# One more feed-forward pair in block form, filter taps joined over two sequences, and a gate in two operations, in a two-layer diffusion backbone on one Trainium2 core

## The chip, the core and the metric

The kernel runs on one core of a Trainium2 chip. A core has a matrix engine (TensorE, PE in the profile; its weight loads are PEld), a vector engine (VectorE, DVE), a scalar engine (ScalarE, ACT), GpSimd (POOL) and SyncE (SP), which here issues most of the transfers. Each engine runs its own list of instructions in order and waits on semaphores for the others. The metric is the time of one execution on the device in microseconds.

## The reference, cut to what matters

One inference step over 128 prompt tokens and 512 sample tokens, width 1024, two layers. The first layer mixes tokens with a state-space scan, the second with differential attention; after each comes the same feed-forward block:

```python
def dwconv(x, w, b):                 # width 3, centred, zero at both ends, each channel by itself
    ...
def conv_ffn(h, up_w, conv_w, conv_b, down_w):
    u = dwconv(h @ up_w, conv_w, conv_b)      # 1024 -> 2 x 2816
    a, v = jnp.split(u, 2, axis=-1)
    return (jax.nn.silu(a) * v) @ down_w      # 2816 -> 1024
...
xp = xp + p_g2 * conv_ffn(modulate(xp, ...), *ffn_p)   # prompt
xs = xs + s_g2 * conv_ffn(modulate(xs, ...), *ffn_p)   # sample, other shift, scale and gate
```

The filter runs over each sequence by itself: the last sample token must not see the first prompt token, nor the other way round.

## The kernel before

Everything is kept transposed: 128 channels on the partitions, 640 tokens in the columns, columns 0 to 511 the sample, 512 to 639 the prompt. Each float32 operand is split into a rounded high part and a remainder (`hi`, `lo`; `whi`, `wlo` for weights, `mh`, `ml` for the hidden tiles), and each product is three matmuls. ScalarE writes the high part, VectorE the low part (`split_w`, line 262). Weights come in units of 128 x 1024 through a ring of buffers: SP loads `raw`, then comes the cast, one to three units ahead of TensorE.

The hidden width is 22 blocks of 128 rows. For each block the kernel computes a pair: the tile `ua` of the first half and `uv` of the second. `FT` is 22, and `SUB` groups the blocks into three stages: the up-projections of a stage and of one block more, then the down-projection of the stage's blocks into eight output tiles (`po`), each added to the residual `x` with its gate. `MID` is the number of buffers for `mh` and `ml` in each layer.

There are two forms of a pair. In the standard form (`pair` in `ffn`) each tile is 8 blocks of 128 input rows, times three matmuls, times two column parts of 256 and 384. In the block form (`Blocks.pair`) the 2 x 2 blocks of weights and activations are combined so that seven products take the place of eight; each is 4 blocks times three matmuls over 320 columns. It needs sums of activations (`Blocks.sums`, tiles `T`) and sums of weights, which GpSimd forms in DRAM by accumulating transfers (`sum_batch`, tensor `wsum`), a batch of blocks at a time, started by `weight_sums`. The products of a pair go into three PSUM banks `a`, `b`, `c`, parts of the tiles named `ba`, `bb` and `bc`. Products 6 and 7 accumulate into the bank of product 1 after ScalarE has copied it out. Products 3 and 4 of a pair are done during the next pair (`third`, `fourth`), and `fourth` ends with the epilogue. `STD` is the number of pairs in standard form: 16 in the first layer, 5 in the second, so 6 and 17 in block form.

The epilogue of a pair filters `ua` into `ca` and `uv` into `cv`, applies SiLU to `ca`, multiplies, and splits the product into `mh` and `ml`. The filter (`conv`, line 677) is one ScalarE operation over 640 columns with the middle tap as scale and the bias, then four VectorE operations: left and right tap, for the sample and for the prompt.

`gate_add` (line 403) adds an output tile to the residual in three VectorE operations, of 256, 256 and 128 columns, because `project_out` calls it for two column parts, "A" and "B", and "B" holds two gates. `project_last` does the last stage's projection and starts the next norm; at the end of a layer it needs the last pair's `mh` and `ml` for its first two tiles' last steps.

In the first layer's feed-forward VectorE also computes the second layer's modulation (`mod_rest`, tiles `mw` and `junk`), which is drained before the down-projection that follows the last standard pair; during that down-projection it makes the sums of activations.

The order on each engine is fixed when the program is built: a list scheduler of the framework takes the instructions in program order as priority, but lets a later one go first if it expects it to be ready sooner.

Of the kernel before, what the change touches and what calls it, by code (L numbers as in the profile page):

```python
# [9 lines left out]
F32 = mybir.dt.float32  # L10
# [16 lines left out]
A0, A1, B1 = 0, 256, 640  # L27
PO = 256
HALF = {"A": (A0, A1), "B": (A1, B1), "C": (0, 384), "D": (384, 640)}
COL0 = {"A": PO, "B": PO, "C": 128, "D": 128}  # L30
COND = {"A": ((0, 256, 1),), "B": ((256, 512, 1), (512, 640, 0)),
        "C": ((0, 384, 1),), "D": ((384, 512, 1), (512, 640, 0))}
# [12 lines left out]
SUMS = 3  # L45
ATT_SPLIT = 6
NF = 19
RSQRT_MAGIC = float(0x5F3759DF)
# [119 lines left out]
class Step:  # L168
# [516 lines left out]
    def ffn(self, l, h, nextnorm, pool):  # L685
# [5 lines left out]
        def copy_out(ps):  # L691
# [2 lines left out]
            self.act(u, ps[:, PO:PO + T], AF.Copy)  # L694
            return u

        def epilogue(p, ua, uv):
            ca = self.tmp("ca")
            self.conv(ca, ua, cw[:, p, :])
            cv = self.tmp("cv")  # L700
            self.conv(cv, uv, cw[:, FT + p, :])
            self.act(ca, ca, AF.Silu)
            self.tt(cv, ca, cv, ALU.mult)
            hi = self.slot("mh", f"mh{p}", F32R, bufs=MID[l], pool=pool)
            lo = self.slot("ml", f"ml{p}", F32R, bufs=MID[l], pool=pool)
# [30 lines left out]
        sub = SUB[l]  # L736
        for s, (k0, k1) in enumerate(sub):
            last = s == len(sub) - 1
            self.down = False
            end = min(k1 + 1, FT)  # L740
            while done < end:
                if done >= std:
                    blk.pair(done)
                else:
                    pair(done)
                    if l and done == 0:
                        sums = self.add(blk.sums(), 2)
                done += 1
                if l == 0 and done == 13:
                    self.weight_sums(1, range(STD[1], 11, SUMS), mid[done - 2][0])  # L750
                if l and done == std:
                    self.drain(sums)
                    blk.finish_sums()
            self.down = True
            if l and s == 0:
                self.weight_sums(1, range(14, FT, SUMS), mid[done - 2][0])
# [561 lines left out]
    def weight_units(self):  # L1318
# [10 lines left out]
        def ffn(l):  # L1329
# [8 lines left out]

            done = 0
            out = []  # L1340
            for k0, k1 in SUB[l]:
# [31 lines left out]

    def weight_sums(self, l, starts, mark):

        for p in starts:
            self.sum_batch(l, p, min(p + SUMS, FT), mark.bitcast(F32)[0:1, 0:2])

    def sum_batch(self, l, p0, p1, mark):

# [147 lines left out]
```

## Time and profile before

| | |
|---|---|
| median of 3 runs | 1868.65 us (1864.55 to 1868.84) |
| profiled execution | 1865.84 us |
| its span, first to last instruction | 1864.1 us |
| TensorE busy | 1827.8 us (98%) |
| VectorE busy | 1464.3 us (79%) |
| ScalarE busy | 998.0 us (54%) |
| GpSimd busy | 55.6 us (3%) |

In the profile a line such as "L217 ACT ACTIVATE ca<-ua,fcw 128x640 f32<-128x640 f32 x23 | 21.1, 918 | 29.5" reads: line 217 of the kernel (a helper that issues all ScalarE operations), engine and operation, tile written and tiles read, shapes, how many; busy microseconds in all and mean nanoseconds of one; idle time of the engine ahead of them and what ended it. Since most operations go through helpers, they are told apart by their tiles.

### The profile page before, as it was taken

To read this page: it belongs to the slowest core of one execution; us is meant where nothing else is said; L and a number is where in the kernel's file an instruction comes from. 1 tells how busy PE (TensorE), PEld (TensorE's weight loads), DVE (VectorE), ACT (ScalarE), POOL (GpSimd) and SP (SyncE) were. 2 spreads that over 40 slices of the span, in tenths; PEclk is the share of its full clock that TensorE was granted. 3 is DMA by queue.
4 is the path that set the end of the run, shared out by engine and by line. 5 is a ranking of instruction groups with operands and counts; after the bars stand their busy time and mean duration, and the time that the engine had idled before them with its cause. 6 is when DMAs were issued, how large, how long until landed. Compare 5 with 4: busy or idle time off the path is not lost.

```text
span 1864.1 us, 33068 instructions
## 1 busy us (share of the span) xinstructions
PE 1827.8 (98%) x13057; PEld 1713.0 (92%) x13057; DVE 1464.3 (79%) x2827; ACT 998.0 (54%) x1862; POOL 55.6 (3%) x84
## 2 busy tenths in 40 slices
PE   7999999999999999999999999999999999999996
PEld 4799999989989999999999988888899999999996
DVE  4689999999838999998585877778779874874874
ACT  2479686879426442345363566566536543643641
POOL 0000000000001000011000000000001011100000
PEclk8999999999999999999999999999999999999998
DMA  9734344345546976677742212111047268853421
GB/s 345 249 115 137 105 120 137 114 132 174 172 162 205 271 236 209 200 209 203 209 128 88 88 40 65 57 46 55 21 124 198 93 181 237 256 161 102 142 80 57
DMA packets 108675, 276.06 MB, mean 148 GB/s; under 512 B 12284, under 2 KB 19048, under 8 KB 102504
## 3 DMA queue, kind: packets, MB, share of 16 engines
q1 hardware_dynamic: 100520, 225.19, 37.1%
q0 software_dynamic: 7424, 48.24, 11.1%
q8 instruction: 102, 1.67, 0.4%
q10 hardware_dynamic: 576, 0.52, 0.1%
q14 instruction: 53, 0.43, 0.1%
HBM read 267.95 MB, written 54.19 MB: 173 GB/s over the span
## 4 chain that ended last, share of the span: by engine, by line
PE 92%; DVE 3%; ACT 2%; DMA 2%; issue 1%; SPq 0%; DVEq 0%; ACTq 0%
PE po L226 25%; PE up L226 14%; PE bb L226 6%; PE z L226 6%; PE ba L226 6%; PE bc L226 5%; PE x L226 5%; PE st L226 5%; PE v L226 3%; PE yp L226 3%; PE q L226 2%; PE sl L226 2%; PE k L226 2%; PE ov L226 2%; PE in L226 1%; PE wt L1252 1%
## 5 line engine op out<-in xcount | busy, mean ns | idle before, releaser
L217 ACT ACTIVATE whi<-raw 128x1024 fp32r<-128x1024 f32 (+4 forms) x266 | 270.9, 1020 | 311.3 <-PE po L226 191.4
L223 DVE TENSOR_TENSOR wlo<-raw,whi 128x1024 fp32r<-128x1024 f32 (+4 forms) x266 | 312.2, 1174 | 74.7 <-ACT whi L217 63.2
L220 DVE SCALAR_TENSOR_TENSOR xr<-po,mod,xr 128x256 f32<-128x256 f32 (+2 forms) x231 | 89.0, 433 | 123.9 <-PE po L226 123.8
L226 PE MATMUL po<-ml,whi 128*128 128x256 f32 (+1 forms) x704 | 168.2, 310 | 0.0
L226 PE MATMUL po<-mh,wlo 128*128 128x256 f32 (+1 forms) x704 | 167.9, 310 | 0.0
L226 PE MATMUL po<-mh,whi 128*128 128x256 f32 (+1 forms) x704 | 167.8, 310 | 0.0
L226 PEld LDWEIGHTS po<-mh,whi 128*128 128x128 f32 x704 | 128.1, 188 | 0.8 <-ACT mh L217 0.5
L226 PEld LDWEIGHTS po<-mh,wlo 128*128 128x128 f32 x704 | 128.7, 188 | 0.0
L226 PEld LDWEIGHTS po<-ml,whi 128*128 128x128 f32 x704 | 128.5, 188 | 0.1
L226 PE MATMUL up<-h01h,wlo 128*128 128x256 f32 x464 | 105.7, 309 | 0.0
L226 PE MATMUL up<-h01l,whi 128*128 128x256 f32 x464 | 105.7, 309 | 0.0
L226 PE MATMUL up<-h01h,whi 128*128 128x256 f32 x464 | 105.6, 309 | 0.0
L226 PEld LDWEIGHTS up<-h01h,whi 128*128 128x128 f32 x464 | 84.4, 188 | 0.0
L226 PEld LDWEIGHTS up<-h01h,wlo 128*128 128x128 f32 x464 | 84.4, 188 | 0.0
L226 PEld LDWEIGHTS up<-h01l,whi 128*128 128x128 f32 x464 | 84.4, 188 | 0.0
L217 ACT ACTIVATE mh<-cv 128x640 fp32r<-128x640 f32 x44 | 32.5, 738 | 88.6 <-DVE cv L223 88.6
L217 ACT ACTIVATE e<-sl,sm 128x640 f32<-128x640 f32 x64 | 50.4, 790 | 39.6 <-DVE sm L1189 39.2
L665 DVE CUSTOM_DVE_ANT_0 junk<-mw,cbc 128x1024 bf16<-128x1024 f32 x48 | 58.4, 1217 | 7.4 <-DMA mw<-in_modT 7.1
L226 PE MATMUL z<-h00h,whi 128*128 128x256 f32 (+1 forms) x256 | 63.0, 325 | 0.0
L217 ACT ACTIVATE e<-rb,Ctok 128x128 f32<-128x128 f32 x160 | 56.4, 390 | 12.0 <-issue 9.6
L217 ACT ACTIVATE ca<-ca 128x640 f32<-128x640 f32 x44 | 32.3, 735 | 54.8 <-DVE ca L220 54.6
L226 PE MATMUL bb<-T,whi 128*128 128x320 f32 x264 | 61.6, 313 | 0.0
(580 smaller groups left out, 5309.9 us busy)
## 6 DMA issues: line engine op xcount, KB each, us to landing
wsum<-in_w_blk POOLq DMA_DIRECT2D x42, 768.0 KB, 7.1
raw<-in_w_blk SPq DMA_DIRECT2D x55, 512.0 KB, 3.9
mw<-in_modT SPq DMA_DIRECT2D x48, 512.0 KB, 4.2
raw<-wsum SPq DMA_DIRECT2D x92, 256.0 KB, 2.9
raw<-in_w_in SPq DMA_DIRECT2D x40, 512.0 KB, 5.3
rb<-rowd SPq DMA_DIRECT2D x40, 512.0 KB, 5.5
raw<-in_w_dn SPq DMA_DIRECT2D x32, 448.0 KB, 3.4
raw<-in_w_qkv SPq DMA_DIRECT2D x24, 512.0 KB, 3.3
```

Source lines behind the costliest of these rows:

```text
L217: return self.nc.scalar.activation(out, in_, func, **k)
L220: return self.nc.vector.scalar_tensor_tensor(out, in0, s, in1, op0, op1)
L223: return self.nc.vector.tensor_tensor(out, a, b, op)
L226: return self.nc.tensor.matmul(out, lhsT, rhs, start=start, stop=stop, **k)
L665: nc.vector.tensor_tensor_reduce(w if c else junk, w, cb[:, c, :], 1.0, 0.0, ALU.mult, ALU.add, self.mod[l][:, t, c:c + 1])
L1252: nc.tensor.transpose(pm[:, b * P:(b + 1) * P], ws[b][:, kc * P:(kc + 1) * P], self.ident)
```

## The change

Four things are edited. In the feed-forward filter the left and the right tap are each one VectorE operation over 639 columns, across the border between sample and prompt. What the two taps add wrongly at the border is taken out beforehand on ScalarE: for each of the two border columns one operation forms the bias less the foreign token's share (`edge`, from negated taps `nw`), and one writes that column of the result anew with it. `project_out` calls the gate once, with a new column set "AB" of two parts, 512 and 128. The first layer has 15 standard pairs and 7 block pairs, with stages of 7, 7 and 8 blocks in both layers and 8 buffers for hidden tiles. The weight sums are batched by explicit bounds: the first layer's seven blocks go in batches of 3, 2 and 2. The filter of the state-space layer keeps its four operations.

```diff
-COL0 = {"A": PO, "B": PO, "C": 128, "D": 128}
+COL0 = {"A": PO, "B": PO, "C": 128, "D": 128, "AB": PO}
 COND = {...
+        ... "AB": ((0, 512, 1), (512, 640, 0))}
-SUB = (((0, 8), (8, 15), (15, 22)), ((0, 7), (7, 14), (14, 22)))
-MID = (9, 8)
+SUB = ((0, 7), (7, 14), (14, 22))
+MID = 8
-STD = (16, 5)
+STD = (15, 5)
...
 def project_out(...):
-            for hf in "AB":
-                self.gate_add(i, ps, g, hf)
+            self.gate_add(i, ps, g, "AB")
...
 def ffn(...):
+        def conv(acc, x, t):
+            w, v = cw[:, t, :], nw[:, t, :]
+            self.act(acc, x, AF.Identity, scale=w[:, 1:2], bias=w[:, 3:4])
+            e = pool.tile([P, 2], F32, tag="edge", name="edge", bufs=4)
+            for i, (a, b) in enumerate(((TS - 1, TS), (TS, TS - 1))):
+                self.act(e[:, i:i + 1], x[:, b:b + 1], AF.Identity, scale=v[:, i:i + 1], bias=w[:, 3:4])
+                self.act(acc[:, a:a + 1], x[:, a:a + 1], AF.Identity, scale=w[:, 1:2], bias=e[:, i:i + 1])
+            self.stt(acc[:, 1:T], x[:, :T - 1], w[:, 0:1], acc[:, 1:T], ALU.mult, ALU.add)
+            self.stt(acc[:, :T - 1], x[:, 1:T], w[:, 2:3], acc[:, :T - 1], ALU.mult, ALU.add)
         def epilogue(p, ua, uv):
-            self.conv(ca, ua, cw[:, p, :])
+            conv(ca, ua, p)
-            self.conv(cv, uv, cw[:, FT + p, :])
+            conv(cv, uv, FT + p)
...
+        nw = pool.tile([P, 2 * FT, 2], F32, tag="nw", name=f"nw{l}", bufs=1)
+        for i in range(2):
+            nc.vector.tensor_scalar(nw[:, :, i], cw[:, :, 2 - 2 * i], -1.0, None, ALU.mult)
-        self.weight_sums(l, range(11, 14, SUMS) if l else range(std, FT, SUMS), h[0][0])
+        self.weight_sums(l, (11, 14) if l else (15, 18, 20, 22), h[0][0])
...
 def weight_sums(self, l, starts, mark):
-        for p in starts:
-            self.sum_batch(l, p, min(p + SUMS, FT), ...)
+        for p, q in zip(starts, starts[1:]):
+            self.sum_batch(l, p, q, ...)
```

More of the change, by code (lines that the diff above doesn't have):

```diff
@@ L29 @@
 HALF = {"A": (A0, A1), "B": (A1, B1), "C": (0, 384), "D": (384, 640)}
-COL0 = {"A": PO, "B": PO, "C": 128, "D": 128}
+COL0 = {"A": PO, "B": PO, "C": 128, "D": 128, "AB": PO}
 COND = {"A": ((0, 256, 1),), "B": ((256, 512, 1), (512, 640, 0)),
-        "C": ((0, 384, 1),), "D": ((384, 512, 1), (512, 640, 0))}
+        "C": ((0, 384, 1),), "D": ((384, 512, 1), (512, 640, 0)), "AB": ((0, 512, 1), (512, 640, 0))}
 EPS = 1e-6
@@ L41 @@
 RAW = 4
-STD = (16, 5)
+STD = (15, 5)
 HT = T // 2
 AHEAD = 3
-SUMS = 3
 ATT_SPLIT = 6
@@ L695, in copy_out @@
             return u
+        def conv(acc, x, t):
[7 more added lines that the diff above has]
+            self.stt(acc[:, :T - 1], x[:, 1:T], w[:, 2:3], acc[:, :T - 1], ALU.mult, ALU.add)
         def epilogue(p, ua, uv):
             ca = self.tmp("ca")
-            self.conv(ca, ua, cw[:, p, :])
+            conv(ca, ua, p)
             cv = self.tmp("cv")
-            self.conv(cv, uv, cw[:, FT + p, :])
+            conv(cv, uv, FT + p)
             self.act(ca, ca, AF.Silu)
             self.tt(cv, ca, cv, ALU.mult)
-            hi = self.slot("mh", f"mh{p}", F32R, bufs=MID[l], pool=pool)
-            lo = self.slot("ml", f"ml{p}", F32R, bufs=MID[l], pool=pool)
+            hi = self.slot("mh", f"mh{p}", F32R, bufs=MID, pool=pool)
+            lo = self.slot("ml", f"ml{p}", F32R, bufs=MID, pool=pool)
             self.act(hi, cv, AF.Copy)
@@ L731, in ffn @@
         nc.vector.tensor_scalar(t, t, -1.0, None, ALU.mult)
+        nw = pool.tile([P, 2 * FT, 2], F32, tag="nw", name=f"nw{l}", bufs=1)
+        for i in range(2):
+            nc.vector.tensor_scalar(nw[:, :, i], cw[:, :, 2 - 2 * i], -1.0, None, ALU.mult)
         sums = None
         self.start_tiles(h)
-        self.weight_sums(l, range(11, 14, SUMS) if l else range(std, FT, SUMS), h[0][0])
+        self.weight_sums(l, (11, 14) if l else (15, 18, 20, 22), h[0][0])
         done = 0
-        sub = SUB[l]
+        sub = SUB
         for s, (k0, k1) in enumerate(sub):
@@ L749, in ffn @@
                 if l == 0 and done == 13:
-                    self.weight_sums(1, range(STD[1], 11, SUMS), mid[done - 2][0])
+                    self.weight_sums(1, (5, 8, 11), mid[done - 2][0])
                 if l and done == std:
@@ L755, in ffn @@
             if l and s == 0:
-                self.weight_sums(1, range(14, FT, SUMS), mid[done - 2][0])
+                self.weight_sums(1, (14, 17, 20, 22), mid[done - 2][0])
             if l == 0 and done == std:
@@ L1340, in ffn @@
             out = []
-            for k0, k1 in SUB[l]:
+            for k0, k1 in SUB:
                 end = min(k1 + 1, FT)
@@ L1374, in weight_sums @@
     def weight_sums(self, l, starts, mark):
-        for p in starts:
-            self.sum_batch(l, p, min(p + SUMS, FT), mark.bitcast(F32)[0:1, 0:2])
+        for p, q in zip(starts, starts[1:]):
+            self.sum_batch(l, p, q, mark.bitcast(F32)[0:1, 0:2])
     def sum_batch(self, l, p0, p1, mark):
```

## The prediction

> **What bounds the kernel now.** I read the page's busy shares first, then busy time by stretch, then the waits of TensorE, then single rows around the edits.
>
> ```profile
> span 1864.1 us, 33068 instructions
> ...
> PE 1827.8 (98%) x13057; PEld 1713.0 (92%) x13057; DVE 1464.3 (79%) x2827; ACT 998.0 (54%) x1862; POOL 55.6 (3%) x84
> ```
>
> TensorE is busy 98% of the span, so an edit pays only if TensorE gets less to do or waits less. The next view sums three stretches: 592 to 693 and 754 to 853 us are standard up pairs of the first feed-forward layer, 907 to 972 us block pairs. Columns: window, its length, then PE, PEld, DVE, ACT and POOL busy with their instructions, clock, DMA share, GB/s.
>
> ```profile
> 592.00:693.00 101.00, 101.00 (x690) 101.00 (x689) 96.28 (x160) 50.59 (x63) 7.63 (x10) 1.00 0.87 264
> 754.00:853.00 99.00, 99.00 (x676) 99.00 (x675) 90.28 (x155) 41.65 (x52) 7.14 (x11) 1.00 0.69 205
> 907.00:972.00 65.00, 64.55 (x429) 62.50 (x428) 48.17 (x74) 37.93 (x55) 0.67 (x1) 1.00 0.51 149
> ```
>
> Three things are to be seen. In the standard stretches TensorE never stops, 101.00/690 = 99.00/676 = 0.1464 us for a matmul, although VectorE is full (96.28 of 101) and the DMA engines too (0.87). So VectorE's load there costs nothing now. In block pairs a matmul takes 65.00/429 = 0.1515 us: a pair of 84 matmuls loses 84 x (0.1515 - 0.1464) = 0.43 us, and ScalarE is at 37.93 of 65 there, VectorE at 48.17. What TensorE waits for in block pairs is mostly a ScalarE copy out of PSUM (total, times, longest):
>
> ```profile
> PEld bb L226 <- ACT ua L217: 3.5, 8, 0.9
> ```
>
> **The change part by part.** *The seventh block pair.* A standard pair is 2 tiles x 8 x 3 x 2 = 96 matmuls of 320 columns on average, 96 x 0.1464 = 14.05 us. A block pair is 7 products x 4 x 3 = 84 matmuls, 84 x 0.1515 = 12.73 us with its losses, 84 x 0.1464 = 12.30 without. Gain 1.32 us, at most 1.75. I take 1.32, since the losses lie in all such pairs. The down-projections keep 22 blocks of 128 rows over three stages, so they keep their matmuls; only 8, 7, 7 becomes 7, 7, 8.
>
> The pair also casts 7 half units of weights (512 columns) where a standard pair casts 4, so 1.5 units more on ScalarE and VectorE. In a stretch with 27 us of 65 free on ScalarE and 17 on VectorE this is hidden. On GpSimd's queue a third batch of weight sums (8 transfers and 2 marks) goes out behind the two that end here:
>
> ```profile
> 669.75 0.87 POOL L1384 DMA_DIRECT2D wsum<-in_w_blk  x1 [6.12 <-DMA wsum<-wsum]
> ```
>
> Two batches took from 566 us to this row, about 52 us each, so the third ends near 730 us even at full size, and its first reader comes after 880. It prolongs the crowded DMA time (0.87 in the first stretch), in which TensorE did not stop. SP issues 6 loads for this pair in place of 2. Nothing.
>
> *The order of stages.* The block stage now begins one standard pair (14.05) and 8 x 6 matmuls (7.0 us) sooner. VectorE must have its modulation sums and the block sums of activations ready that much sooner.
>
> ```profile
> 832.95 1.22 DVE L665 CUSTOM_DVE_ANT_0 mw<-mw,cbc 128x1024 f32<-128x1024 f32 x1
> ```
>
> ```profile
> 890.00:900.00 10.00, 4.53 (x8) 1.00 0.85 234
> ```
>
> ```profile
> 902.98 0.30 PE L226 MATMUL ba<-h01h,whi 128*128 128x320 f32 x1
> ```
>
> The last modulation sum ran at 833 us, the activation sums kept VectorE full till about 894.5 us (the second row: VectorE 4.53 of 10), and the first block product came at 902.98: 8.4 us to spare. TensorE will reach the down stage ahead of it at 853 - 21 = 832 us. Even if the modulation sums end no sooner, VectorE enters 2 us behind, within 8.4. Nothing; if that cover were gone, the start of the block stage would slip by what is over.
>
> *Taps over 639 columns.*
>
> ```profile
> L220 DVE SCALAR_TENSOR_TENSOR ca<-ua,fcw,ca 128x511 f32<-128x511 f32 x46 | 34.4, 747 | 12.9 <-ACT ca L217 12.9
> ...
> L220 DVE SCALAR_TENSOR_TENSOR w<-e,sm,e 128x640 f32<-128x640 f32 x32 | 28.1, 880 | 8.6 <-ACT e L217 8.5
> ...
> L220 DVE SCALAR_TENSOR_TENSOR ca<-ua,fcw,ca 128x127 f32<-128x127 f32 x46 | 15.9, 346 | 0.0
> ```
>
> Four operations, 2 x 747 + 2 x 346 = 2186 ns, become two of about 880 (the middle row, one column more). Successive VectorE operations overlap by some 80 ns (four taps last 1.93 us in a row below), so 1.85 becomes 1.60: 0.25 us less for each of 88 filters, 22 us of VectorE in all. It ends no wait of TensorE that the waits name, so by itself it is worth nothing.
>
> *Border columns on ScalarE.* Each filter gets four operations on one column, 88 x 4 = 352 in all. The trace has none of that shape with scale and bias taken from memory.
>
> ```profile
> L217 ACT ACTIVATE uraw<-up 128x640 f32<-128x640 f32 x36 | 24.7, 686 | 0.0
> ...
> L217 ACT ACTIVATE ca<-ua,fcw 128x640 f32<-128x640 f32 x23 | 21.1, 918 | 29.5 <-DVE ua L223 29.5
> ...
> L217 ACT ACTIVATION_READ_ACCUMULATOR e<-sl,sm 128x1 f32 x64 | 12.5, 195 | 0.0
> ...
> L217 ACT ACTIVATE wpT<-wpt 128x128 f32<-128x128 f32 x8 | 2.2, 276 | 0.0
> ```
>
> A column costs (686 - 276)/512 = 0.80 ns, so the filter's own 640-column operation, which has the same two operands, shrinks to 918 - 639 x 0.80 = 407 ns at one column. Less the 0.09 us by which ScalarE operations overlap (0.91 long, 0.82 apart, below) that is 0.31 us in a row. The low end is the one-column row, 195 ns, 0.10 with the overlap; the high end 0.41, if each waits for the one before it, as every second one needs the first's result. I take 0.31, which is of the same kind: 1.24 us a filter, 2.5 a pair, 109 us in all.
>
> The Trainium skill, "ScalarE: Activation LUTs", section "What ACT_TABLE_LOAD costs", gives 186 ns plus about 93 for each operand in memory and 93 of overlap, by which (an estimate) such an operation takes 0.28 us and a pair 2.2; the sum would stay within 0.1 us.
>
> In standard pairs ScalarE has half its time free. In block pairs five pairs lie in 65 us, so its 37.93 becomes 50.6: still below the limit, and I put the steady part at nothing. Its bounds: a gain of 0.43 for each of 23 block pairs (9.9 us), if the waits vanished, and the loss of the first rival.
>
> The cover is gone at the end of a layer, where the last pair's hidden tile is the only thing that TensorE still needs:
>
> ```profile
> 1797.39 0.92 ACT L217 ACTIVATE cv<-uv,fcw 128x640 f32<-128x640 f32 x1
> 1798.22 0.72 ACT L217 ACTIVATE ca<-ca 128x640 f32<-128x640 f32 x1
> 1801.73 0.74 ACT L217 ACTIVATE mh<-cv 128x640 fp32r<-128x640 f32 x1 [2.78 <-DVE cv L223]
> ```
>
> ```profile
> 1798.83 1.93 DVE L220 SCALAR_TENSOR_TENSOR cv<-uv,fcw,cv 128x511 f32<-128x511 f32 x4
> ```
>
> ```profile
> 1802.09 1.30 PE L226 MATMUL po<-mh,whi 128*128 128x256 f32 x6
> ```
>
> The tile `mh` is written at 1801.73 to 1802.47 and TensorE takes it just then. VectorE's taps for `ca` will start 1.24 us later and last 0.25 less, a cast comes between, the taps for `cv` start 1.0 later and last 0.25 less: `mh` comes 0.75 us late, and TensorE with it (bounds 0 and 2.5). In the first layer six more matmuls (0.88 us) now lie ahead of that point, so 0. The two earlier ends of stages in the second layer have cover:
>
> ```profile
> 1511.20 0.82 DVE L223 TENSOR_TENSOR ml<-cv,mh 128x640 fp32r<-128x640 f32 x1
> ```
>
> ```profile
> 1507.97 6.29 PE po L226 x42
> ```
>
> `ml` is done at 1512.0; the last six of these 42 matmuls begin at 1507.97 + 36/42 x 6.29 = 1513.4 and reach `ml` 0.3 later. 1.6 us of cover against 0.75: nothing, or 0.4 each if `ca`'s columns also hold up the copy of `uv`.
>
> *Gate in two operations* for 45 tiles: one operation fewer, its fixed part (346 - 127 x 1.04 = 213 ns, less overlap 0.13 us) on VectorE, behind matmuls that do not wait for it. Nothing. The two small operations for negated taps, once a layer, neither.
>
> **Sum:** -1.32 + 0.75 = -0.6 us. The profiled execution took 1865.84 us (span 1864.1 and 1.7 around it), so 1865.2. It lies 2.8 us under the median of the three runs, by which the sum is 1868.0; I forecast the middle, 1866.6. A difference under 0.3% (5.6 us) cannot be told from none in this kernel.
>
> **The rivals.** *Slower: ScalarE's columns stand ahead of a copy that TensorE needs.* In the second layer's steady pairs:
>
> ```profile
> 1742.85 0.42 ACT L217 ACTIVATE uv<-ba 128x320 f32<-128x320 f32 x1
> 1743.17 0.91 ACT L217 ACTIVATE ca<-ua,fcw 128x640 f32<-128x640 f32 x1
> 1743.99 0.91 ACT L217 ACTIVATE cv<-uv,fcw 128x640 f32<-128x640 f32 x1
> 1744.80 0.41 ACT L217 ACTIVATE ua<-bb 128x320 f32<-128x320 f32 x1
> ```
>
> ```profile
> 1746.06 0.31 PE L226 MATMUL bb<-h11h,whi 128*128 128x320 f32 x1
> ```
>
> The copy `ua<-bb` frees the bank into which the product at 1746.06 goes; it ends at 1745.21, 0.85 us early. Eight columns ahead of it in ScalarE's queue are 2.5 us: TensorE stops 1.6 us. Every second pair has this order, 11 of 23: +18 us, 1884. With four columns ahead, 0.4 x 11 = 4 us, 1871. It decides from 0.5 us of stop in 11 pairs. For it: the slack is one row. Against it: the order is made when the program is built, the copy comes earlier in the program than the columns, so it may go between them. The Trainium skill, same page, section "Rules for kernel authors", sends adds and multiplies to VectorE and budgets some 0.3 us for an operation on ScalarE; by that rule (an estimate) the move is a loss of this kind, and no run here shows it yet.
>
> *Faster: the waits in block pairs go.* If shorter taps freed VectorE's and ScalarE's buffers sooner, half the 0.43 us of 23 pairs would come back, 5 us: 1861.6; all of it 1856.7. Against: the waits name ScalarE's copies, and ScalarE gets more to do.
>
> *The seventh pair brings nothing:* its sums or loads come late and cost the 1.32 us: 1867.9, no change all the same.
>
> **How the numbers follow.** Forecast 0.55, the third case 0.08 (both within 0.3%), slower rival 0.22, faster rival 0.15. So faster 0.15, same 0.63, slower 0.22. The range goes from the faster case's half-way toward all (1859) to a slower case between four and eight columns (1877); that leaves out about 1 in 10. The likeliest alone has 1863 to 1870.
>
> **What would show it.** Right: the first layer has 588 block matmuls in place of 504 and 96 fewer `up`; one-column ScalarE rows near 0.4 us; taps near 880 ns; ScalarE near 1140 us busy (998 + 352 x 0.4), VectorE near 1420 (1464 less 88 x 0.43 and 45 x 0.1); a wait of `po` for `mh` at the end of the second layer of up to 1 us. Wrong: waits of `ba` or `bb` for ScalarE's `ua` far above 3.5 us, a stop before the first block product, or a matmul in block pairs nearer 0.1464 us.

## The result, and the profile after

The changed kernel takes 1878.41 us (median, 1877.56 to 1881.89); the kernel before took 1866.88 on the same chip (1863.62 to 1868.84). The ratio is 1.0066, with an interval from 1.0056 to 1.0077: 11.5 us slower. The forecast was 1866.6, no change, with a range up to 1877. The profiled execution took 1878.28 us.

The page of the changed kernel opens so:

```profile
span 1876.5 us, 33203 instructions
...
PE 1828.7 (97%) x13045; PEld 1711.7 (91%) x13045; DVE 1443.7 (77%) x2615; ACT 1092.0 (58%) x2218; POOL 62.1 (3%) x94
```

TensorE is as long busy as before, 0.9 us more, in a span that is 12.4 us longer: it stops. To find where, I take the first matmul of each normalisation, `st`, on the feed-forward's input (`h01h`), on the attention's (`h10h`) and on the second feed-forward's (`h11h`), and the end of the span. These are starts of single rows, 569.1, 1031.3 and 1399.4 us before, 570.1, 1042.0 and 1409.8 after.

| Stretch | before | after |
|---|---|---|
| first feed-forward (`h01h` to `h10h`) | 462.2 | 471.9 |
| attention (`h10h` to `h11h`) | 368.1 | 367.8 |
| second feed-forward (`h11h` to the end) | 464.7 | 466.7 |

So 9.7 us of the loss lie in the first feed-forward and 2.0 in the second. The waits of TensorE in the first, from 560 to 900 us (total, times, longest), a view that is empty for the kernel before:

```profile
PE po L225 <- ACT mh L216: 4.8, 2, 3.2
PE po L225 <- DVE ml L222: 1.6, 1, 1.6
PE po L225 <- DVE xr L219: 1.5, 1, 1.5
PE po L225 <- ACT uraw L216: 0.5, 1, 0.5
```

These are 8.4 us, all of `po`, the down-projection, and most for hidden tiles, `mh` and `ml`. In the timeline of TensorE they stand at the first down-projection (692 and 694 us) and at the second. The second begins 16 us sooner than it did; its first row before:

```profile
853.18 0.45 PE L226 MATMUL po<-mh,whi 128*128 128x256 f32 x2
```

and after, with the longest stop:

```profile
837.22 0.56 PE L225 MATMUL po<-mh,whi 128*128 128x256 f32 x2 [0.50 <-ACT uraw L216]
...
845.95 0.90 PE L225 MATMUL po<-mh,whi 128*128 128x256 f32 x2 [3.19 <-ACT mh L216]
```

The same hidden tile on VectorE, from the timeline of that engine:

```profile
826.94 0.88 DVE L219 SCALAR_TENSOR_TENSOR cv<-uraw,fcw,cv 128x639 f32<-128x639 f32 x1
831.89 1.22 DVE L663 CUSTOM_DVE_ANT_0 junk<-mw,cbc 128x1024 bf16<-128x1024 f32 x1 [4.06 <-DMA mw<-in_modT]
833.04 0.82 DVE L222 TENSOR_TENSOR cv<-ca,cv 128x640 f32<-128x640 f32 x1
...
834.92 1.22 DVE L663 CUSTOM_DVE_ANT_0 junk<-mw,cbc 128x1024 bf16<-128x1024 f32 x1
...
836.06 0.82 DVE L222 TENSOR_TENSOR ml<-cv,mh 128x640 fp32r<-128x640 f32 x1
836.80 0.88 DVE L219 SCALAR_TENSOR_TENSOR ca<-uraw,fcw,ca 128x639 f32<-128x639 f32 x1
...
842.41 1.80 DVE L219 SCALAR_TENSOR_TENSOR cv<-uraw,fcw,cv 128x639 f32<-128x639 f32 x2 [0.63 <-ACT cv L216]
...
845.93 0.83 DVE L222 TENSOR_TENSOR ml<-cv,mh 128x640 fp32r<-128x640 f32 x1 [0.86 <-ACT mh L216]
```

VectorE has the second tap of `cv` done at 827.8 and the gated half `ca` has been there since 822.6 (ScalarE's timeline below, under e4). But the next instruction in its queue is a modulation reduction, and its tile of weights, `mw`, lands only at 831.9. VectorE stands still for 4.06 us with the hidden tile's work behind it. The load itself was issued only at 827.1 us, when VectorE had read out one of the two buffers of `mw` (a reduction from 825.80, 1.22 us long), and took 4.8 us; the median of the run is 4.5. Two hidden tiles follow, at 836.1 and 845.9, and TensorE, which has been at this stage since 837.2, needs the second one 3.2 us before it is there.

All such waits from 560 to 900 us, first before, then after:

```profile
DVE junk L665 <- DMA mw<-in_modT: 7.1, 3, 3.4
```

```profile
DVE junk L663 <- DMA mw<-in_modT: 20.5, 11, 4.1
```

And the first down-projection's surroundings, 670 to 720 us (columns as in the prediction: window, length, PE, PEld, DVE, ACT, POOL busy, clock, DMA share, GB/s), before and after:

```profile
670.00:720.00 50.00, 50.00 (x340) 50.00 (x339) 49.77 (x89) 19.87 (x25) 0.61 (x1) 1.00 0.63 199
```

```profile
670.00:720.00 50.00, 46.88 (x318) 46.36 (x317) 44.58 (x71) 18.47 (x33) 3.61 (x5) 1.00 0.80 223
```

After, the DMA engines are at 0.80 instead of 0.63 there, POOL still issues weight-sum copies (3.61 us against 0.61), and VectorE does less, 44.58 of 50 us, because it waits for `mw`.

A last part of the loss is the clock. Five-microsecond windows around the 3.2 us stop:

```profile
840.00:845.00 5.00, 2.77 (x19) 2.50 (x17) 4.29 (x5) 2.38 (x6) 0.00 (x0) 1.00 0.95 157
845.00:850.00 5.00, 4.05 (x16) 3.69 (x17) 2.70 (x4) 4.09 (x8) 1.17 (x2) 0.66 0.74 265
850.00:855.00 5.00, 5.00 (x36) 5.00 (x35) 3.25 (x5) 3.78 (x7) 0.00 (x0) 1.00 0.93 327
```

Just behind the stop the granted clock is 0.66 and TensorE gets 16 matmuls done in 4.05 us, where full clock (the row below: 36 in 5.00) makes 29: some 13 matmuls or 1.8 us more.

### The profile page after: what moved, and what is told of

It is laid out like the page before. It is cut to its first block, busy times and chain, and to the rows that moved or that the text cites. A ratio compares the mean times of both kernels' runs of the same rounds, so it can differ in the third digit from the quotient of the medians.

```text
span 1876.5 us, 33203 instructions
## 1 busy us (share of the span) xinstructions
PE 1828.7 (97%) x13045; PEld 1711.7 (91%) x13045; DVE 1443.7 (77%) x2615; ACT 1092.0 (58%) x2218; POOL 62.1 (3%) x94
## 3 DMA queue, kind: packets, MB, share of 16 engines
q0 software_dynamic: 7872, 50.34, 11.5%
## 4 chain that ended last, share of the span: by engine, by line
PE 77%; DVE 10%; DMA 6%; ACT 5%; issue 2%; SPq 0%; DVEq 0%; ACTq 0%
PE po L225 22%; PE ba L225 6%; PE z L225 6%; PE x L225 5%; PE bb L225 5%; PE bc L225 5%; PE st L225 4%; DMA mw<-in_modT 4%; PE v L225 3%; PE yp L225 3%; PE up L225 3%; PE k L225 2%; PE sl L225 2%; PE q L225 2%; DVE wlo L222 2%
## 5 line engine op out<-in xcount | busy, mean ns | idle before, releaser
L219 DVE SCALAR_TENSOR_TENSOR xr<-po,mod,xr 128x128 f32<-128x128 f32 (+3 forms) x186 | 83.2, 487 | 116.7 <-PE po L225 116.7
L225 PE MATMUL up<-h01h,whi 128*128 128x256 f32 (+1 forms) x432 | 98.4, 309 | 0.0
L225 PE MATMUL up<-h01h,wlo 128*128 128x256 f32 (+1 forms) x432 | 98.4, 309 | 0.0
L225 PE MATMUL up<-h01l,whi 128*128 128x256 f32 (+1 forms) x432 | 98.4, 309 | 0.0
L219 DVE SCALAR_TENSOR_TENSOR ca<-ua,fcw,ca 128x639 f32<-128x639 f32 x48 | 42.4, 884 | 48.9 <-ACT ca L216 48.1
L225 PEld LDWEIGHTS up<-h01l,whi 128*128 128x128 f32 x432 | 78.6, 188 | 0.0
L225 PEld LDWEIGHTS up<-h01h,whi 128*128 128x128 f32 x432 | 78.6, 188 | 0.0
L225 PEld LDWEIGHTS up<-h01h,wlo 128*128 128x128 f32 x432 | 78.5, 188 | 0.0
L663 DVE CUSTOM_DVE_ANT_0 junk<-mw,cbc 128x1024 bf16<-128x1024 f32 x48 | 58.6, 1220 | 20.6 <-DMA mw<-in_modT 20.5
```

What stands on the lines that cost most here:

```text
L219: return self.nc.vector.scalar_tensor_tensor(out, in0, s, in1, op0, op1)
L225: return self.nc.tensor.matmul(out, lhsT, rhs, start=start, stop=stop, **k)
L663: nc.vector.tensor_tensor_reduce(w if c else junk, w, cb[:, c, :], 1.0, 0.0, ALU.mult, ALU.add, self.mod[l][:, t, c:c + 1])
```

## The experiments

The theory, A: late `mw` loads hold up hidden tiles in VectorE's queue. In its narrower form, A1, the loads are late because of the weight-sum copies on GpSimd's queue, which now come in three batches. Rivals: B, the border columns on ScalarE; A2 and D, the weights' own stream and the earlier second down-projection; C, the taps by themselves, and the gate. All medians, with the ratio to the kernel before on the same chip in brackets and the first feed-forward of the profiled execution, as in the table above. A profiled execution need not be near its median: those of e7 and e10, 1873.1 and 1872.4 us, are the longest of theirs, and that of e4, 1868.2, is among the shorter. The before's median lay between 1866.1 and 1867.3. The waits are those from 560 to 900 us.

| Kernel | us (ratio) | first feed-forward | VectorE's waits for `mw` |
|---|---|---|---|
| before | 1866.9 | 462.2 | 7.1 |
| after | 1878.4 (1.0056 to 1.0077) | 471.9 | 20.5 |
| e1 joined taps alone | 1870.1 (1.0015 to 1.0035) | 466.8 | 9.9 |
| e2 seventh pair alone | 1873.1 (1.0029 to 1.0060) | 472.6 | 19.1 |
| e3 after, modulation not loaded | 1865.5 (0.9984 to 1.0003) | 460.4 | none |
| e4 after, no border columns | 1871.6 (1.0013 to 1.0037) | 463.5 | 13.5 |
| e5 after, sums early | 1866.0 (0.9992 to 1.0010) | 461.7 | 10.2 |
| e6 before, sums early | 1868.2 (0.9996 to 1.0018) | 462.3 | 2.9 |
| e7 seventh pair, sums early | 1867.7 (0.9998 to 1.0020) | 463.9 | 11.2 |
| e8 gate alone | 1865.8 (0.9986 to 1.0005) | 462.3 | 8.1 |
| e9 after, sums early, no columns | 1864.7 (0.9983 to 1.0000) | 460.4 | 5.3 |
| e10 after, sums early, columns on VectorE | 1866.3 (0.9992 to 1.0010) | 460.2 | 3.5 |
| e11 after, third batch early | 1871.5 (1.0020 to 1.0042) | 465.3 | 13.7 |
| e12 before, with after's three batches | 1866.9 (1.0003 to 1.0021) | 462.2 | 10.4 |
| e13 after, modulation work sooner | 1875.7 (1.0035 to 1.0074) | 477.2 | 15.9 |
| e14 after, sums early, modulation sooner | 1866.3 (0.9985 to 1.0003) | 460.4 | 6.9 |

**e1, the joined taps alone.** In the kernel before:

```diff
-            self.conv(ca, ua, cw[:, p, :])
+            conv(ca, ua, p)        # two taps over 639 columns, no border operations
```

> The kernel before with the joined taps over 639 columns only; the border columns are not put right, so ScalarE gets nothing new; 16 standard pairs, old stages, gate in three operations. Theory A (in the first layer VectorE's queue stands behind late modulation loads, and the stages' ends, now 21 us sooner, meet hidden tiles that are not ready): no loss, 1864 to 1868 us, as the stages have not moved. Theory B (ScalarE's border columns delay the epilogues): the same, 1864 to 1868. Theory C (shorter taps alone let VectorE run into the modulation loads): 1870 or more, with waits of VectorE for mw near 20 us.

1870.1 us, 3.8 more than before, where theories A and B had no loss; C had the time, but not the waits (near 20 us). The run has a first feed-forward of 466.8. TensorE stops at the first down-projection for a hidden tile, of which the kernel before shows nothing:

```profile
PE po L226 <- DVE ml L223: 1.7, 1, 1.7
PE po L226 <- ACT mh L217: 1.1, 1, 1.1
```

So shorter work on VectorE, by itself, cost time. The waits for `mw` rose from 7.1 to 9.9 us, and 4.0 of these lie between 670 and 720 us, just ahead of that down-projection, against none in the kernel before. The order in VectorE's queue differs too: the eighth `ml`, for which TensorE stops, is written from 707.6 us, behind 19 of the 48 `junk` reductions, and before from 696.9 us, behind 17. Why the scheduler put more of them ahead was not tried.

**e2, the seventh block pair alone**, with its stages and its third batch of sums, the old taps and the old gate.

```diff
 (the changed kernel)
-            conv(ca, ua, p)
+            self.conv(ca, ua, cw[:, p, :])
...
-            self.gate_add(i, ps, g, "AB")
+            for hf in "AB":
+                self.gate_add(i, ps, g, hf)
```

> The seventh block pair, the new stages and the third batch of weight sums only; taps in four operations, gate in three, no border columns. Theory A: the loss in the first layer stays, 1874 to 1880 us, with TensorE waiting some 3 us each for mh in the down-projections of stages 1 and 2 of the first layer. Theory B: no loss, 1863 to 1867.

1873.1, 6.8 more than before and just under theory A's 1874 to 1880. Its waits from 560 to 900 us:

```profile
PE po L225 <- ACT uraw L216: 3.4, 2, 2.2
PE po L225 <- DVE xr L219: 3.3, 1, 3.3
PE po L225 <- ACT mh L216: 1.2, 1, 1.2
PE po L225 <- DVE ml L222: 0.6, 1, 0.6
```

The names differ, the place does not: `xr` is the gate of the down-projection on VectorE, and the copy `uraw` of the next up tile stands in ScalarE's queue behind work that waits for VectorE (in e2 at 848.97 us, behind an operation on `ca` that had waited 7.19 us; in the changed kernel at 845.81, behind an `mh` from 845.16). An engine that is late shows up under whichever of its outputs is needed next. The part that was to bring 1.3 us is the largest loss of those measured alone.

**e3, the changed kernel without the modulation loads.** Two tiles of weights are loaded and all 96 reductions read these, so the second layer's modulation is that of the first two tiles again and again; the reductions keep their number and size (all of them write `junk`).

```diff
-            if t < 47:
+            if t < 1:
                 nxt = pool.tile([P, 1024], F32, tag="mw", name="mw", bufs=2)
                 nc.sync.dma_start(nxt, a["modT"][t + 1])
+                two.append(nxt)
+            elif t < 47:
+                nxt = two[(t + 1) % 2]
...
```

> The changed kernel, with only two of the 48 tiles of modulation weights loaded and the same reductions run over those two (layer 1's modulation is computed from wrong weights). VectorE's work stays, its waits for mw go. Theory A: the 9.7 us that the first layer lost go, 1866 to 1869 us. Theory B: no change, 1877 to 1879. If VectorE's work rather than the loads makes the hidden tiles late: 1874 to 1878.

1865.5 us: everything comes back, just under theory A's 1866 to 1869. The window of the second stop:

```profile
840.00:880.00 40.00, 40.00 (x276) 40.00 (x275) 30.38 (x57) 12.64 (x21) 4.38 (x6) 1.00 0.81 216
```

TensorE does not stop in it, with the same reductions, border columns and copies. That the loss hangs on the `mw` loads is shown. As they also move data, this run alone doesn't say whether their lateness or their traffic is at fault; the waits point to their lateness.

**e4, the changed kernel without the border columns** (the two columns at the border keep what the taps add across it).

```diff
-            e = pool.tile([P, 2], F32, tag="edge", name="edge", bufs=4)
-            for i, (a, b) in enumerate(((TS - 1, TS), (TS, TS - 1))):
-                self.act(e[:, i:i + 1], ...)
-                self.act(acc[:, a:a + 1], ...)
```

> The changed kernel without the four border operations on ScalarE in each filter (border columns left wrong), about 100 us of ScalarE less. Theory A: 1875 to 1878 us, only the about 2 us that the second layer lost come back. Theory B: 1864 to 1868.

1871.6, so the columns are worth 6.8 us of the changed kernel's time, which neither theory had (A 1875 to 1878, B 1864 to 1868). e4 holds the pair, the taps and the gate, and loses 5.3 us, less than e2 and e1 added up: the parts have no price each of their own. In its second feed-forward, 464.2 us in the profile, they account for these waits of block products, which were 1.3 and 0.5 us in the kernel before. After:

```profile
PE bb L225 <- ACT uv L216: 1.8, 4, 0.5
PE ba L225 <- ACT ua L216: 1.3, 1, 1.3
...
PE ba L225 <- ACT uv L216: 0.5, 1, 0.5
PE bb L225 <- ACT ua L216: 0.2, 1, 0.2
```

And in e4:

```profile
PE bb L225 <- ACT ua L216: 1.5, 4, 0.5
PE ba L225 <- ACT uv L216: 0.5, 1, 0.5
```

3.8 against 2.0 us: that is some 2 us of the price; the rest is in the first feed-forward, 463.5 against 471.9 in single profiles. ScalarE's timeline of the changed kernel ahead of the long stop:

```profile
821.89 0.74 ACT L216 ACTIVATE ca<-ca 128x640 f32<-128x640 f32 x1 [2.67 <-DVE ca L219]
...
826.01 0.93 ACT L216 ACTIVATE ca<-uraw,fcw 128x640 f32<-128x640 f32 x1
833.89 0.74 ACT L216 ACTIVATE mh<-cv 128x640 fp32r<-128x640 f32 x1 [6.95 <-DVE cv L222]
834.53 0.65 ACT L216 ACTIVATE edge<-uraw,fcw,nw 128x1 f32<-128x1 f32 x2
835.09 0.65 ACT L216 ACTIVATE ca<-uraw,edge,fcw 128x1 f32<-128x1 f32 x2
```

The middle tap of the next filter is done at 826.9, but its border columns stand behind `mh<-cv`, which waits 6.95 us for VectorE, which waits for the load. So the next taps on VectorE can't begin before 835.7; without the columns they would need nothing of ScalarE after 826.9. One late load is passed on to a second queue. In this place it was not yet what counted: the taps begin at 836.80, right behind `ml` in VectorE's own queue, without a wait. What VectorE does wait for the columns in this stage is 0.63 us at the most, at 842.41 (0.45 in e4, without columns). From 560 to 900 us its waits for ScalarE's `ca` and `cv` are 2.7 and 0.6 us, in the changed kernel as in e5, which loses nothing. How the columns add to the first stage's stops is not shown.

**e5, the first layer's sums in the scan stage**, where the DMA engines of the changed kernel are at 0.28 to 0.50 of their time (150 to 400 us, by stretches of 50).

```diff
 def ssd(...):
             bcs[g] = bc
+            if g == 1:
+                self.weight_sums(0, (15, 18, 20, 22), bc[0])
 def ffn(...):
-        self.weight_sums(l, (11, 14) if l else (15, 18, 20, 22), h[0][0])
+        if l:
+            self.weight_sums(1, (11, 14), h[0][0])
```

> The changed kernel with one thing moved: the three batches of weight sums of the first layer are issued during the scan stage (after the second group of input tiles) instead of at the start of the feed-forward, and nothing else differs. Theory A1 (the third batch's copies keep the DMA engines at 0.79 instead of 0.56 of their time from 680 to 720 us, and so make VectorE's modulation tiles late): VectorE's waits for these tiles fall from 20.5 us to below 7, TensorE no longer waits for the hidden tiles, and the time falls from 1878.4 to 1867-1871; the border columns' 2 us of the second layer stay. Theory A2 (the tiles are late because of the weight stream itself and the lighter or earlier VectorE work, the copies do not matter): waits stay above 14 us, 1875-1881.

1866.0 us: 12 us come back by moving copies alone. The same window as above, 670 to 720 us:

```profile
670.00:720.00 50.00, 50.00 (x346) 50.00 (x345) 49.71 (x83) 18.36 (x30) 0.00 (x0) 1.00 0.63 196
```

The DMA share is 0.63 instead of 0.80, and VectorE works 49.71 of 50 us. The waits for `mw` fell less far than A1 had said, to 10.2 us and not below 7. But they fell just where the copies had been. The changed kernel issues its last one at 699.8 us; its waits from 560 to 720 us, a view that is empty for e5:

```profile
DVE junk L663 <- DMA mw<-in_modT: 11.5, 5, 3.9
```

From 720 to 900 us they are 8.9 us, and 10.2 in e5. The loads issued from 560 to 680 us land after 5.4 us (median) beside the copies and after 4.2 in e5. So VectorE falls behind early and carries this on. Each tile of weights has two reductions, `junk` and `mw`; the fifteenth `junk` of 48, after and in e5:

```profile
687.46 1.22 DVE L663 CUSTOM_DVE_ANT_0 junk<-mw,cbc 128x1024 bf16<-128x1024 f32 x1 [3.85 <-DMA mw<-in_modT]
```

```profile
675.97 1.22 DVE L663 CUSTOM_DVE_ANT_0 junk<-mw,cbc 128x1024 bf16<-128x1024 f32 x1
```

The gap is 11.5 us here and still 11.5 us at the last one (834.92 against 823.41 us). The 4.06 us at 831.9 us are thus not the copies' work: e5 waits at the same reduction, 4.58 us, but there it comes when there is room:

```profile
820.38 1.23 DVE L663 CUSTOM_DVE_ANT_0 junk<-mw,cbc 128x1024 bf16<-128x1024 f32 x1 [4.58 <-DMA mw<-in_modT]
...
834.42 0.82 DVE L222 TENSOR_TENSOR ml<-cv,mh 128x640 fp32r<-128x640 f32 x1 [0.86 <-ACT mh L216]
```

The stage's last hidden tile begins to be written at 834.4, and TensorE starts the stage at 831.7: 2.7 us behind it. After, the two stand at 845.9 and 837.2, 8.7 us behind. TensorE has six hidden tiles to go through, 36 matmuls or some 5 us, before it comes to the last one. So a wait by itself says little; how late the last hidden tile is against the start of its down-projection says it.

**e6, the same move in the kernel before.**

```diff
 def ssd(...):
+            if g == 1:
+                self.weight_sums(0, range(16, FT, SUMS), bc[0])
... (and out of ffn, as in e5)
```

> The kernel before with the same move of its two batches of weight sums to the scan stage. It shows what the move does by itself. Theory A1 and A2 alike: TensorE has no stop there to win back, so 1864-1868, with the 7.1 us of VectorE's waits for modulation tiles falling to under 4 by A1 and staying by A2. If the batches disturb the scan stage instead, over 1869.

1868.2, no change that can be told (0.9996 to 1.0018), with 2.9 us of waits for `mw`. The kernel before had no stop to win back, so the move by itself brings nothing.

**e7, the seventh pair alone with the sums early.**

```diff
 (e2)
+            if g == 1:
+                self.weight_sums(0, (15, 18, 20, 22), bc[0])
... (and out of ffn, as in e5)
```

> The seventh block pair alone (old taps, old gate: 1873.1 before this) with its three batches of weight sums issued during the scan stage. Theory A1: its 19.1 us of waits for modulation tiles fall below 7, and it comes to the kernel before less the 1.3 us of the seventh pair, 1864-1867. Theory A2: 1871-1875. A third way: the waits go, but TensorE still waits for the hidden tiles of 15 VectorE-heavy pairs before the block stage, 1868-1871.

1867.7, between A1's 1864 to 1867 and the third way's 1868 to 1871, with waits of 11.2 us and not below 7: of e2's 6.8 us, 1.5 are left, which can't be told from none. With the old, longer taps VectorE is busy 308.65 us from 560 to 900, against 302.69 in e5, and one stop of 2.7 us for `xr` stays.

**e8, the gate alone.**

```diff
-            for hf in "AB":
-                self.gate_add(i, ps, g, hf)
+            self.gate_add(i, ps, g, "AB")
```

> The kernel before with the gate of the split projections in two operations instead of three, nothing else. Every theory: no change by itself, 1864-1868. Over 1869 it would be a part of the loss that the theories have left out, under 1862 a gain.

1865.8: nothing, as forecast.

**e9, e5 without the border columns** (the two columns are left out as in e4).

```diff
 (e5)
-            for i, (a, b) in enumerate(((TS - 1, TS), (TS, TS - 1))):
-                self.act(e[:, i:i + 1], ...)
-                self.act(acc[:, a:a + 1], ...)
```

> The changed kernel with the first layer's weight sums issued in the scan stage (1866.0 us so far) and the border columns left out (the two columns at the border of sample and prompt stay wrong; every other instruction is there). Theory B (the border columns on ScalarE cost about 2 us in the second feed-forward, 466.7 us with them against 464.2 without): 1863.3-1865.0, about 2 us below the same kernel with them, and 1.3 us or more below the kernel before by the seventh pair. Rival (the difference of the second feed-forward is scatter of single profiles, or the seventh pair brings nothing): 1865.4-1867.

1864.7, as theory B had it, but its interval (0.9983 to 1.0000) overlaps that of e5: 1.3 us are about what can be told. Against 6.8 us in e4 it shows that most of the columns' price was not theirs but that of the stops.

**e10, the border columns on VectorE.**

```diff
 (e5)
-                self.act(e[:, i:i + 1], x[:, b:b + 1], ...)
-                self.act(acc[:, a:a + 1], x[:, a:a + 1], ...)
+                self.stt(acc[:, a:a + 1], x[:, b:b + 1], v[:, i:i + 1], acc[:, a:a + 1], ALU.mult, ALU.add)
```

> The same, with the border columns put right by two one-column operations of VectorE instead of four of ScalarE (176 in all). The nearest rows give one such operation 0.06 to 0.3 us, estimated from the shorter taps, so VectorE gets 10 to 50 us more over both layers. Theory B: ScalarE's chain ahead of the block products is as short as without the columns, and the second feed-forward keeps 464-465 us; in the first one VectorE has the modulation work too, and what it loses there decides: 1863.5-1866.0 at 0.06-0.15 us each. Rival: at 0.3 us each VectorE falls behind in the first feed-forward and TensorE waits for hidden tiles again, 1868-1874.

1866.3, the same as e5 and just above B's 1863.5 to 1866.0. From the groups by shape, one of these operations:

```profile
L219 DVE SCALAR_TENSOR_TENSOR cv<-uv,nw,cv 128x1 f32<-128x1 f32 x48 | 9.1, 214 | 0.0
```

176 of them are about 32 us of VectorE, within the 10 to 50 that were expected, and TensorE waits for none of them. Which engine does the columns makes no difference that can be measured.

**e11, the changed kernel with the third batch alone early.**

```diff
 def ssd(...):
+            if g == 1:
+                self.weight_sums(0, (20, 22), bc[0])
 def ffn(...):
-        self.weight_sums(l, (11, 14) if l else (15, 18, 20, 22), h[0][0])
+        self.weight_sums(l, (11, 14) if l else (15, 18, 20), h[0][0])
```

> The changed kernel with only the third batch of weight sums of the first layer (pairs 20 and 21) issued in the scan stage; the first two stay at the start of the feed-forward. Theory A1, third batch alone: the DMA share of 680 to 720 us falls from 0.79 to near 0.56, the waits for modulation tiles from 20.5 to 8-14 us, and the time to 1866-1870. Rival (all three batches crowd the queue, the first two delay the tiles as well): waits 14-20 us, 1872-1878.

1871.5, between the two and above the 1866 to 1870 expected: about 7 of 12 us. From 670 to 720 us:

```profile
670.00:720.00 50.00, 50.00 (x346) 50.00 (x345) 49.58 (x81) 19.20 (x33) 0.00 (x0) 1.00 0.62 192
```

The first stop is gone with the third batch's copies. The second remains: the last hidden tile is written from 839.2, TensorE starts that stage at 832.9, 6.3 us ahead. The first two batches thus put VectorE behind too: from the tenth on, its `junk` reductions run 4.5 to 5.9 us behind those of e5.

**e12, the kernel before with the changed kernel's three batches** (the sums of pair 15 are written and not used).

```diff
+            for p0, p1 in ((15, 18), (18, 20), (20, 22)):
+                self.sum_batch(0, p0, p1, h[0][0].bitcast(F32)[0:1, 0:2])
... (in place of the two batches; the tensor of sums begins at pair 15)
```

> The kernel before with the changed kernel's three batches of weight-sum copies (pairs 15 to 21, in batches of three, two and two) in place of its two batches; the sums of pair 15 are written and not used, nothing else differs. Theory A1 with the copies alone as cause: VectorE's waits for modulation tiles rise from 7.1 to over 14 us, TensorE waits for hidden tiles, 1869-1874. Rival A3 (the copies need the earlier block stage to do harm: with one more pair and an older tap order there is slack): the waits rise, but the time stays at 1865-1868.

1866.9, 1.0003 to 1.0021: the rival A3 holds. The copies alone, without the earlier stages, cost 0.6 to 3.9 us by the interval, and TensorE does not stop for them:

```profile
670.00:720.00 50.00, 50.00 (x339) 50.00 (x339) 48.05 (x87) 20.05 (x25) 2.21 (x3) 1.00 0.69 215
```

The waits rise to 10.4 us and TensorE works through. e2 has these very copies and one thing besides, the seventh pair with its stages, and loses 6.8 us. In e12 the first down-projection starts at 695.2 us and in e2 at 681.5, and the second, in the kernel before, at 853.2, in the changed one at 837.2. From 560 to 720 us VectorE waits 8.2 us for `mw` in e12 and 8.1 in e2, the copies being the same, and none in e6 and 0.7 in e7, without them there (the old taps in all four). So the copies set this lateness, with the pair or without it, and the pair's loss takes both: copies that make the loads late, and down-projections that come sooner.

**e13, the modulation work let go sooner.**

```diff
-            self.modtask = self.add(self.mod_rest(1, 0, pool), 48)
+            self.modtask = self.add(self.mod_rest(1, 0, pool), 8)
```

> The changed kernel with one number changed: the modulation work of VectorE is let go 8 ticks after the start of the first feed-forward instead of 48, at the same pace of 7 ticks for a reduction; all copies stay where they are. Theory D (the second down-projection comes 16 us sooner than before, so that the modulation work ends too near to it: last hidden tile 845.9 us, TensorE there from 837.2): the last reduction, 834.9 us before, comes some 10 to 25 us sooner, the hidden tile is there in time, the 5 us of stops from 837 to 865 us go, and the time falls to 1867-1872; the 3 us at 692 us stay or grow. Rival (the tiles' loads are bound by the copies, an earlier start only adds to the crowd): last reduction still within 6 us of 834.9, 1875-1881.

1875.7, within the rival's 1875 to 1881; the interval overlaps that of the changed kernel. The profiled execution (1881.6) is the second longest of its seven. In it the second stage's waits shrink to one of 1.4 us, but a new stop of 7.4 us comes earlier:

```profile
PE up L225 <- DVE wlo L222: 7.4, 1, 7.4
```

VectorE splits the `up` weights (`wlo`), and with the modulation work in front of them from the start, TensorE waits for these. The last `junk` reduction is at 836.3 (834.9 in the changed kernel), within the rival's 6 us, where D expected it 10 us sooner. So D in the form "more time for the modulation work" is not shown: the work ran into the crowd earlier and hurt there.

**e14, both moves.**

```diff
 (e5)
-            self.modtask = self.add(self.mod_rest(1, 0, pool), 48)
+            self.modtask = self.add(self.mod_rest(1, 0, pool), 8)
```

> The changed kernel with both: weight sums of the first layer in the scan stage and the modulation work let go at 8 ticks. Theory A1 with D: no wait of TensorE for hidden tiles in the first feed-forward, which takes 460-461 us as it does without the loads, and 1864.5-1866.5 in all, about 1 us at most below the 1866.0 with the sums moved alone. Rival: the earlier modulation work delays the first tiles of the feed-forward, 1867-1870.

1866.3. TensorE has no wait from 560 to 900 us, the last reductions start at 820.0 and 821.9 us and the first feed-forward is 460.4 us long. This is where the change's gain of that stage can be read. No version beats the kernel before by more than can be told: e5, e10 and e14, which compute all of it, lie at 0.9992 to 1.0010, 0.9992 to 1.0010 and 0.9985 to 1.0003.

## Why the prediction was wrong, step by step

**The order of stages, "Nothing": this step failed.** It counted the 21 us by which the block stage comes sooner, weighed them against the 8.4 us of room ahead of the first block product, and stopped there. But the down-projection of the second stage comes sooner as well, 837.2 instead of 853.2 us, and it needs hidden tiles that stand in VectorE's queue among the modulation reductions. That queue was read for its last reduction (833 us before; 837.6 after, 0.4 behind TensorE and within the 8.4) and not for the hidden tiles that stand among the reductions, nor for the 11.5 us by which the copies put it behind. The Trainium skill, "PSUM — Partial Sum Buffer", section "Engine vs sequencer instructions", says that the queues of ScalarE and VectorE are strictly first in, first out; the 4.06 us on VectorE and the 6.95 us on ScalarE above, with ready work behind each, agree. The first block product now starts at 893.2 us; the prediction's 21 us, with the later start of the feed-forward by 1.0, would have it at 882.9. First row after, second row e5, the tile's total over the view:

```profile
L225 PE MATMUL ba<-h01h,whi x48: 304/309/417, 893.2 to 979.4; 128*128 128x320 f32 x48
```

```profile
L225 PE MATMUL ba<-h01h,whi x48: 305/309/417, 882.2 to 968.4; 128*128 128x320 f32 x48
```

With the sums early it is at 882.2, so the 21 us were right and 10 of them were lost on the way: the term put at nothing was worth some 10 us.

**The third batch on GpSimd's queue: the sentence "it prolongs the crowded DMA time, in which TensorE did not stop" was the second half of the same fault.** The copies do prolong it (0.80 instead of 0.63). That TensorE did not stop in crowded time before was true of standard pairs, and the rows that showed it ended at 693 us, ahead of the first down-projection (698.2). The crowd ended sooner than forecast, with a last copy at 699.8 us and not near 730; the harm lay in the delay that VectorE carried on. e12 shows the sentence right for the kernel before, e5 and e11 wrong for this one.

**The seventh pair, -1.32:** in the three profiles that compute everything or leave only columns out, and have no stop of TensorE in that stretch (e9, e10, e14), the first feed-forward takes 460.2 to 460.4 us against 462.2: -1.8 to -2.0 in single profiles, with the taps and the gate in it. Right in sign and near in size.

**Taps at 880 ns, worth nothing:** they take 879 to 884. Alone they cost 3.8 us (e1), with another order in VectorE's queue; the prediction had no term for that.

**Border columns at 0.31 us in a row:** each lasts 374 ns, and in ScalarE's timeline pairs of them start 0.56 us apart, 0.28 for one:

```profile
1744.27 0.65 ACT L216 ACTIVATE edge<-uv,fcw,nw 128x1 f32<-128x1 f32 x2
1744.83 0.65 ACT L216 ACTIVATE cv<-uv,edge,fcw 128x1 f32<-128x1 f32 x2
```

By the figures in the Trainium skill, "ScalarE: Activation LUTs", section "What ACT_TABLE_LOAD costs", an estimate gave 0.28, and this trace agrees. ScalarE's busy time was put at 1140 us and is 1092.0, since two back to back count 0.65 and not 0.8.

**The slower rival** came near the total (1871 and 1884 for 1878.4) by luck, with a wrong mechanism. It put eight columns ahead of a bank copy. The trace of the changed kernel in the steady pairs shows the copy going between them:

```profile
1741.88 0.38 ACT L216 ACTIVATE edge<-ua,fcw,nw 128x1 f32<-128x1 f32 x1
1742.29 0.44 ACT L216 ACTIVATE uv<-bb 128x320 f32<-128x320 f32 x1
1742.62 0.38 ACT L216 ACTIVATE ca<-ua,edge,fcw 128x1 f32<-128x1 f32 x1
```

That was the argument against it, and it held. The waits of block products in the second layer rose by 2.0 us in place of 4 to 18, mostly once, at the first block pairs. The same page's section "Rules for kernel authors" sends such adds to VectorE. By e10 against e5 that brings nothing here that can be measured.

**End of the second layer, +0.75:** TensorE's weight load waits 0.3 us for `mh` there, and 0.2 before: too high, in its bounds. **Gate, nothing:** right (e8).

What stays open: why the joined taps alone move VectorE's reductions ahead of a hidden tile, how the border columns add to the stops of the first feed-forward, and whether the earlier down-projections harm by the time that the modulation work has, as e13 did not separate this.

## What to carry to other kernels

When stages are moved up, check every consumer that moves with them, and for each the whole queue of the engine that feeds it: an instruction that waits for a load holds up all behind it, however ready that is. A transfer that is "hidden" is so only against the deadlines as they stand; with both the transfers and the deadlines changed, price the two together. Compare when the last tile is written with when its consumer starts, rather than the waits: one of 4.58 us cost nothing in e5, one of 4.06 us stands ahead of the 3.2 us stop in the changed kernel. And look far back for the cause: the delay that stopped TensorE at 842 us had been built up before 700.

## What the runs showed of the hardware

The granted clock of TensorE fell to 0.66 in the five microseconds behind a stop of 3.2 us, and to 0.87 on the mean of 600 to 640 us in e13 with its stop of 7.4, while a stop of 1.5 us (the window at 860 to 865 us) left it at 1.00; a long stop so costs more than its own length. The Trainium skill, "TensorE: Matmul & The Clock Gate", section "Why this matters for your kernels", asks for no gap over some 3 us; the stops of 3.2 and 7.4 us agree. Shorter ones were not always safe here: behind 2.75 us in e7 the clock was 0.80 (855 to 860 us), and behind two stops of 1.1 and 1.7 us close together in e1 it was 0.72 (710 to 715), while 2.57 us in e11 and the two of 1.6 us at 692 and 694 us in the changed kernel left it at 1.00. An operation over one column takes 0.37 us alone on ScalarE and 0.21 on VectorE.
